# A bias on four token tiles: by matmul or by accumulating transfer, and a shorter form of one scalar step in the norms

## The chip, the cores and the metric

The kernel runs on one core of a Trainium2 chip. The metric is the device time of one execution in microseconds (us). A profile is one such execution taken by the hardware profiler. Its span, from the first to the last instruction, is a little shorter than the execution's own time.

The core has five engines, each with its own queue of instructions in a fixed order: TensorE (PE in the profile; its weight loads are PEld), VectorE (DVE), ScalarE (ACT), GpSimd (POOL) and SyncE (SP). SyncE here issues plain transfers. GpSimd issues the transfers that add to what stands at their destination ("accumulating"). All transfers share 16 DMA engines.

## The reference

One decoder layer over 1024 tokens of width 1024 in fp32: a pooling mixer and a gated feed-forward net with a short convolution, each behind an RMS norm and added to the residual.

```python
def pool_mixer(x, w, b, scale):            # windows 2, 4, 8, 16, one per group of 256 channels
    ...
        groups.append(window_sum / count - xf[..., gi * POOL_GROUP:(gi + 1) * POOL_GROUP])
    d = jnp.stack(groups, axis=2)
    y = jnp.einsum('bsgc,gcd->bsgd', d, w.astype(jnp.float32)).reshape(bsz, seq, D_MODEL) + b
    return (scale * y).astype(x.dtype)

def reference(x, ...):
    h = rms_norm(x, norm_mix_g[layer])
    y = pool_mixer(h, pool_w[j], pool_b[j], pool_scale[j])
    x = x + y.astype(x.dtype)
    f = conv_ffn(rms_norm(x, norm_ffn_g[layer]), ffn_w_in[layer], ffn_conv_w[layer], ffn_conv_b[layer], ffn_w_out[layer])
    x = x + f.astype(x.dtype)
```

What matters here: the mixer adds `scale * b`, the same row of 1024 numbers for every token, to the residual x.

## The kernel before

**Tiles.** The 1024 tokens are 8 tiles of 128 tokens (j = 0 to 7), each a 128 x 1024 fp32 tile `xs[j]` with tokens in the partitions. For each j the mixer stage does, in this order:

- `stat(j)` (through `rstd_of`): ScalarE squares and sums the row (L178, out `junk_a`) and takes a root (L179); VectorE refines it in three steps on one column (L180, L182, L183). L182 computes root * root + ms, with root and ms a column each.
- `mixer_norm(j)`: VectorE scales the four window matrices by that norm (L187, `bandr`).
- `mixer_window(j)` or `window_sums(j)`: 8 matmul calls on `xs[j]` and `bandr` give the window sums, turned so that channels are in the partitions (L201, `psd`). VectorE adds the edges from the tile before (L270), and ScalarE copies the sums out as `dh` (L271).
- `mixer_out(j)`: 8 matmul calls of `dh` with the scaled pool weights `wps` (L286, out `psy`), and two of a tile of ones with `bias_hl`, which holds the scaled bias as a high and a low part in its rows 0 and 1 (L289). VectorE adds x in place (L292, `x1 = psy + x`), SyncE stores x1 to DRAM (L293), and the second norm's `rstd_of` follows (`junk_b`, `st_b`).
- `ffn_norm(j)`: VectorE applies the second norm (L304, out `n`).
- `ffn_operand(j)`: TensorE transposes the result (L319, `pst`); ScalarE and VectorE write it out as high and low parts (L328 to L339).

The fp32 matmul calls of L201 and L286 show as two matmuls each in the profile; the transposes of L319 and the calls on fp32r data (L289, L402) show as one.

**The feed-forward product** is a Strassen-like scheme of seven products per hidden tile n, 22 tiles (L402, banks X, Y, Z). Its weight tile `raws[n]` holds four blocks a11, a12, a21, a22 (`win` in the profile). For each n the scheme needs the sums S3 = a11 + a21, S1 = a21 + a22 (written to a21), S2 = a11 + S1 (written to a11) and S4 = a12 + S2 (written to a12). `sums_in` (L358 to L373) makes them by accumulating transfers on GpSimd (L361, 256 KB each); for n = 0 and 1 it is called with step 0 (S3, S1) and with step 1 (S2, S4). Each operand is split into two parts by ScalarE (L91) and VectorE (L92) before TensorE uses it. From the end of the mixer stage until about 465 us TensorE does these products, then the last product of the layer.

**The order.** Instructions run on each engine in an order fixed when the program is built. It follows the order of the code where operands are ready, and `tc.issue_after(m)` puts a block's instructions behind instruction m in its engine's queue. The loop over j (L527 to L557) holds the mixer's steady part: at step j it issues the window of tile j - 1, the output of tile j - 2, the second norm of j - 2 and the transposes of j - 4. `sums_in(n, 0)` is called at steps 4 and 6, `sums_in(n, 1)` at steps 7 and 8.

**Buffers.** `x_edge`, the 128 rows at the tile edges, is a 128 x 1024 tile with the tag "ha" (one buffer). It is last read by the matmuls of `mixer_edges`. The next user of "ha" is `ha0`, which the products of n = 0 fill.

Of the kernel before, what the change touches and what calls it, by code (L numbers as in the profile page):

```python
# [7 lines left out]
F32 = mybir.dt.float32  # L8
# [3 lines left out]
ALU = mybir.AluOpType  # L12
PSUM = bass.MemoryType.PSUM

P = 128
S = 1024
D = 1024
# [22 lines left out]
NOPS_A = 3  # L40

XBUFS = 5

PAD = 24

# [18 lines left out]
def trunk_kernel(ctx: ExitStack, tc: tile.TileContext, x, consts, par, rows, pool_w, w_in, w_out, out):  # L64
    nc = tc.nc

    const = ctx.enter_context(tc.tile_pool(name="const", bufs=1))
    dram = ctx.enter_context(tc.tile_pool(name="dram", bufs=1, space=bass.MemoryType.DRAM))
# [4 lines left out]
    work = ctx.enter_context(tc.tile_pool(name="work", bufs=1, side="right"))  # L73
# [6 lines left out]
    def bank2(name):  # L80
        return ps_p.tile([P, 2 * NH], F32, tag="ps", name=name)
# [16 lines left out]
    xs = {}  # L98

    def load_x(j):  # L100
        if j < 2 or j >= 2 + XBUFS:
            xs[j] = hls.tile([P, D], F32, tag="hl", name=f"x{j}", bufs=7)
        else:
            xs[j] = pp.tile([P, D], F32, tag="x", name=f"x{j}", bufs=XBUFS)
        for cols in HALVES if j == 0 else [slice(0, D)]:
            nc.sync.dma_start(xs[j][:, cols], x[j * P : (j + 1) * P, cols])
# [28 lines left out]
    for g, w in enumerate(WINDOWS):  # L135

        m = band[:, g, :]
# [30 lines left out]
    def rstd_of(src, name, halves=False):  # L168
        junk = pp.tile([P, D], BF16, tag="junk", name=f"junk_{name}")
        st = pp.tile([P, 8], F32, tag="st", name=f"st_{name}", bufs=8)  # L170
        part, first, ms, root, q, inv, half = (st[:, i : i + 1] for i in range(7))
        bias = eps_t
        if halves:
            bias = first
            nc.scalar.activation(junk[:, :NH], src[:, :NH], AF.Square, accum_out=half)
            nc.vector.tensor_scalar(first, half, D * EPS, None, op0=ALU.add)
            src, junk = src[:, NH:], junk[:, NH:]
        nc.scalar.activation(junk, src, AF.Square, accum_out=part)  # L178
        marks[name] = nc.scalar.activation(root, part, AF.Sqrt, bias=bias).ins  # L179
        nc.vector.tensor_scalar(ms, part, first if halves else D * EPS, None, op0=ALU.add)  # L180

        nc.vector.scalar_tensor_tensor(q, root, root, ms, op0=ALU.mult, op1=ALU.add)  # L182
        nc.vector.reciprocal(inv, q)  # L183
        return root, inv

# [8 lines left out]
    def mixer_norm(j):  # L194
        t = bands[j] = pp.tile([P, NG, P], F32, tag="bandr", name=f"bandr{j}", bufs=2)
        for groups in [slice(0, 2), slice(2, 4)] if j == 0 else [slice(0, NG)]:
            marks[f"band{j}"] = normed(t[:, groups, :], (band if j else band0)[:, groups, :], stats[j])

    def windows(ps, src, weights):
        for c in range(NK):  # L200
            m = nc.tensor.matmul(ps[:, c * P : (c + 1) * P], src[:, c * P : (c + 1) * P], weights[:, c // 2, :], start=True, stop=True)  # L201
        return m.ins
# [13 lines left out]
    wps = pp.tile([P, 2 * NG, GRP], F32, tag="wps", name="wps")  # L216
# [13 lines left out]


    b8 = rows8[:, 1, :]

    def pool_bias():
        marks["bias"] = nc.scalar.activation(bias8[:, 0, :], b8, AF.Copy).ins
        marks["bias_dve"] = nc.vector.tensor_tensor(bias8[:, 1, :], b8, bias8[:, 0, :].bitcast(F32), ALU.subtract).ins
        for l in range(2):
            m = nc.sync.dma_start(bias_hl[l : l + 1, :].bitcast(F32), bias8[:, l, :].bitcast(F32)).ins
        with tc.issue_after(m):
            for j in range(3, NS):  # L240
                load_x(j)
            nc.sync.dma_start(par_sb[:, :GM], par[:, :GM])
# [14 lines left out]
    def window_sums(j):  # L257
        ps = bank2(f"psd{j}")
        marks[f"psd{j}"] = windows(ps, xs[j], bands.pop(j))
        return ps  # L260

    def mixer_window(j, ps=None):
        ps = window_sums(j) if ps is None else ps
        dh = ds[j] = pp.tile([P, NK, P], F32, tag="dh", name=f"dh{j}", bufs=2)
        ps3 = ps.rearrange("p (c s) -> p c s", c=NK)
        first = ps3[:, :, :HALO]
        if j == 0:
            marks["first"] = nc.vector.tensor_tensor(first, first, fac, ALU.mult).ins
        elif j > 1:
            nc.vector.tensor_tensor(first, first, edges[:, :, j * HALO : (j + 1) * HALO], ALU.add)  # L270
        marks[f"dh{j}"] = nc.scalar.activation(dh, ps3, AF.Copy).ins  # L271
# [9 lines left out]
    def mixer_out(j, stats=True):  # L281
        dh = ds.pop(j)
        ps = bank2(f"psy{j}")
        for c in range(NK):
            o = ps[:, c // 2 * GRP : (c // 2 + 1) * GRP]
            nc.tensor.matmul(o, dh[:, c, :], wps[:, c, :], start=c % 4 == 0, stop=False, skip_group_check=True)  # L286
        for h in range(2):
            cols = slice(h * NH, (h + 1) * NH)
            m = nc.tensor.matmul(ps[:, cols], ones, bias_hl[:, cols], start=False, stop=True, skip_group_check=True)  # L289
        marks[f"psy{j}"] = m.ins  # L290
        x1 = n2s[j] = xs.pop(j)
        marks[j] = nc.vector.tensor_tensor(x1, ps, x1, ALU.add).ins  # L292
        nc.sync.dma_start(x1_dram[j * P : (j + 1) * P, :], x1)  # L293
        if stats:
            mixer_out_stats(j)

    def mixer_out_stats(j):
        n2s[j] = (n2s[j], rstd_of(n2s[j], f"b{j}"))

    def ffn_norm(j):  # L300
        x1, r = n2s[j]
        n2 = n2s[j] = pp.tile([P, D], F32, tag="n2", name=f"n2_{j}", bufs=2)
        nc.vector.tensor_tensor(r[1], r[0], r[1], ALU.mult)
        marks[f"n{j}"] = nc.vector.scalar_tensor_tensor(n2, x1, r[1], gains[0], op0=ALU.mult, op1=ALU.mult).ins  # L304
# [50 lines left out]
    def tmp(name):  # L355
        return work.tile([P, NH], F32, tag="sum", name=name, bufs=3)

    def sums_in(n, step):  # L358

        def more(out, a):  # L360
            nc.gpsimd.dma_start(out, a, accum_op=ALU.add)  # L361

        a11, a12, a21, a22 = (raws[n][:, i, k * NH : (k + 1) * NH] for i in range(2) for k in range(2))
        if step == 0:
            s3 = sums[n, "S3"] = tmp(f"S3_{n}")
            nc.sync.dma_start(s3, w_in[order[n]][:, 0, :NH])
            more(s3, a21)
            more(a21, a22)
        else:
            sums[n, "S2"] = a11  # L370
            more(a11, a21)
            sums[n, "S4"] = a12
            more(a12, a11)  # L373
# [95 lines left out]
    def prep_event(k):  # L469
        if k < len(events):  # L470
            n, p = events[k]
            prep_in(n, STEPS[p][0])
# [49 lines left out]
        mixer_edges()  # L522
    with tc.issue_after(marks["edges_pe"]):
        sums3 = window_sums(3)
    with tc.issue_after(marks["dh1+"]), tc.issue_after(marks["edges"]):
        mixer_out_stats(0)
    for j in range(2, NS + 4):  # L527
        if 3 < j < NS:
            with tc.issue_after(marks[1]) if j == 4 else nullcontext():
                mixer_norm(j)  # L530
        if 1 <= j - 1 < NS and j > 2:
            mixer_window(j - 1, {3: sums2, 4: sums3}.get(j))
        if j == NS + 1:
            with tc.issue_after(marks[f"n{NS - 2}"]):
                prep_event(4)
                prep_event(6)
        if 1 <= j - 2 < NS:
            with tc.issue_after(marks["S4", 0] if j == NS + 1 else marks[f"band{min(j, 4)}"]) if j > 2 else nullcontext(), tc.issue_after(marks["psd3"]):
                mixer_out(j - 2)
        if 0 <= j - 2 < NS:  # L540
            with tc.issue_after(marks["dh1+"]):
                ffn_norm(j - 2)
        if 0 <= j - 4 < NS:
            ffn_operand(j - 4)
        if j in (4, 6):
            load_in(j // 2 - 2)
            sums_in(j // 2 - 2, 0)
        if 5 <= j <= 8:
            with tc.issue_after(marks[j - 2]), tc.issue_after(marks[f"b{j - 3}"]):
                prep_event(j - 5)  # L550
        if j in (7, 8):
            sums_in(j - 7, 1)
        if j in (8, 10, 11):
            event((8, 10, 11).index(j))
        with tc.issue_after(marks["edges"]):
            stat(j + 1)
            stat(j + 2)  # L557
# [156 lines left out]
    for k in range(-SLOOK, len(oevents)):  # L714
        p, f = oevents[k + SLOOK] if k + SLOOK < len(oevents) else (None, 0)
# [8 lines left out]
        with tc.issue_after(lasts[-1]) if lasts else nullcontext():  # L724
# [12 lines left out]
            p, f = oevents[k]  # L737
# [10 lines left out]
        if f == 0 and opens:  # L748
            for i in range(4):
                tag = ("XXYY" if set_ == "X" else "YZZZ")[i]  # L750
# [15 lines left out]
        for i, g, c, bank in steps:  # L766
            a, b = oops[p, g]
            alone = opens and (p, i) != ("P4", 3)
            for m, (u, v) in enumerate(((0, 0), (0, 1), (1, 0))):
# [3 lines left out]
                    start=opens and first, stop=g == NP2 - 1 and m == 2, skip_group_check=not alone,  # L773
# [83 lines left out]
```

## Time and profile before

| | us |
|---|---|
| median of 3 runs | 672.28 |
| lowest, highest | 670.89, 673.64 |
| profiled execution, its own time | 670.79 |
| its span | 669.0 |

The TensorE clock that was granted is full speed over the whole span. The rows of the page, of the chain of waits and of the timelines stand in the prediction, where they are used. In a row of a timeline the columns are: start, duration (both us), engine, line, operation, out <- in, shapes, count; in square brackets, how long the engine was idle before it and what released it. In a row of the chain they are: start, duration, engine, tile, line, count. In a row of groups, behind the count, stand the busy time in us, the mean duration of one in ns, and the idle time before them with what ended it. In a row of the windows they are the stretch, its length, and the busy time and count of PE, PEld, DVE, ACT and POOL, then the granted clock, the DMA share and GB/s.

Some stretches of the mixer stage, from the view by windows:

| stretch, us | PE | DVE | ACT | DMA share |
|---|---|---|---|---|
| 20 to 30 | 10.00 | 5.80 | 7.27 | 0.97 |
| 30 to 40 | 10.00 | 9.57 | 8.08 | 0.91 |
| 40 to 50 | 10.00 | 9.26 | 9.53 | 0.82 |
| 50 to 60 | 10.00 | 8.38 | 7.96 | 0.38 |
| 60 to 70 | 10.00 | 9.34 | 5.97 | 0.32 |

### The profile page before, as it was taken

The numbers are of one execution on the slowest core, as the hardware profiler recorded it, in microseconds if no ns is written. First come the engines' busy times: TensorE is split into PE (matmuls) and PEld (weight loads), VectorE is DVE, ScalarE is ACT, GpSimd is POOL, SyncE is SP. The second block draws the span as 40 slices with busy tenths as digits, with TensorE's granted clock in tenths as the row PEclk, the third lists the DMA queues.
The fourth block names the chain that finished last, engine by engine and source line by source line (L and its number), as shares of the span: only waits on it lengthen the run. The fifth ranks groups of instructions, "written<-read, shape, count | busy, mean of one in ns | idle before, by whom it ended". The sixth has DMA issues, their size and how long they took to land.

```text
span 669.0 us, 8720 instructions
## 1 busy us (share of the span) xinstructions
PE 663.6 (99%) x3164; PEld 579.2 (87%) x3164; DVE 569.1 (85%) x841; ACT 338.8 (51%) x517; POOL 47.8 (7%) x73
## 2 busy tenths in 40 slices
PE   9999999999999999999999999999999999999997
PEld 7999878888888888888888888888888888888886
DVE  4798999998888888888888888887987988999995
ACT  6696656554544544444544454454554444444441
POOL 3021020111001111111011101100000000000000
PEclk9999999999999999999999999999999999999999
DMA  8983253544444454544444444429999710232231
GB/s 269 326 207 105 85 141 126 167 145 124 133 134 105 123 142 141 143 130 128 135 141 130 113 136 132 111 92 350 332 335 352 269 58 0 62 96 82 62 125 64
DMA packets 41603, 101.23 MB, mean 151 GB/s; under 512 B 4668, under 2 KB 6616, under 8 KB 38744
## 3 DMA queue, kind: packets, MB, share of 16 engines
q1 hardware_dynamic: 34464, 87.55, 37.3%
q0 software_dynamic: 6944, 12.59, 11.3%
q10 hardware_dynamic: 152, 0.53, 0.3%
q8 instruction: 25, 0.41, 0.2%
q14 instruction: 18, 0.15, 0.1%
HBM read 68.14 MB, written 19.92 MB: 132 GB/s over the span
## 4 chain that ended last, share of the span: by engine, by line
PE 96%; DVE 2%; ACT 1%; issue 0%; POOL 0%; ACTq 0%; POOLq 0%
PE oP L771 29%; PE Y L402 25%; PE X L402 17%; PE Z L402 16%; PE psy L286 4%; PE psd L201 2%; PE pst L319 1%; DVE T L339 1%; PE psy L289 1%; PE ps_scale L222 0%; PE idle_ps L149 0%; DVE n2f L580 0%; ACT B L338 0%; PE ps_edges L201 0%; PE ps_gain L248 0%
## 5 line engine op out<-in xcount | busy, mean ns | idle before, releaser
L771 PE MATMUL oP<-oBP,oAP 128*128 128x512 f32 (+1 forms) x924 | 198.9, 378 | 0.1
L771 PEld LDWEIGHTS oP<-oBP,oAP 128*128 128x128 f32 x924 | 174.0, 189 | 25.0 <-DVE oBP L92 0.5
L402 PE MATMUL X<-B,A11s 128*128 128x512 f32 x264 | 61.5, 380 | 0.0
L402 PE MATMUL Y<-T,S3s 128*128 128x512 f32 x264 | 60.8, 380 | 0.4 <-DVE q L431 0.4
L402 PE MATMUL Y<-T,A22s 128*128 128x512 f32 x264 | 60.8, 380 | 0.0
L402 PE MATMUL Z<-T,S1s 128*128 128x512 f32 x264 | 60.8, 379 | 0.0
L402 PE MATMUL X<-B,A12s 128*128 128x512 f32 x264 | 60.6, 379 | 0.0
L402 PE MATMUL Y<-T,S2s 128*128 128x512 f32 x264 | 60.6, 379 | 0.0
L402 PE MATMUL Z<-B,S4s 128*128 128x512 f32 x264 | 60.5, 379 | 0.0
L402 PEld LDWEIGHTS Y<-T,S3s 128*128 128x128 f32 x264 | 49.7, 189 | 8.2 <-DVE q L431 1.2
L402 PEld LDWEIGHTS Y<-T,A22s 128*128 128x128 f32 x264 | 49.7, 189 | 7.9 <-DVE hb L439 0.6
L402 PEld LDWEIGHTS Z<-T,S1s 128*128 128x128 f32 x264 | 49.8, 189 | 7.5 <-DVE T L339 0.4
L402 PEld LDWEIGHTS Z<-B,S4s 128*128 128x128 f32 x264 | 49.8, 189 | 7.3 <-DVE r L436 0.3
L402 PEld LDWEIGHTS Y<-T,S2s 128*128 128x128 f32 x264 | 49.9, 189 | 7.1
L402 PEld LDWEIGHTS X<-B,A11s 128*128 128x128 f32 x264 | 49.7, 189 | 7.3 <-DVE A11s L92 0.4
L402 PEld LDWEIGHTS X<-B,A12s 128*128 128x128 f32 x264 | 49.8, 189 | 7.0
L91 ACT ACTIVATE oBP<-blk 128x512 fp32r<-128x512 f32 x53 | 33.1, 625 | 44.2 <-PE oP L771 30.6
L460 ACT ACTIVATE gate<-gate 128x1024 f32<-128x1024 f32 x22 | 23.2, 1057 | 49.3 <-DVE gate L451 49.3
L91 ACT ACTIVATE oAP<-blk 128x512 fp32r<-128x512 f32 x55 | 34.1, 620 | 19.3 <-DVE blk L350 16.8
L92 DVE TENSOR_TENSOR oBP<-blk,oBP 128x512 fp32r<-128x512 f32 x53 | 36.5, 688 | 8.6 <-ACT oBP L91 6.6
L92 DVE TENSOR_TENSOR oAP<-blk,oAP 128x512 fp32r<-128x512 f32 x55 | 37.7, 685 | 2.6 <-ACT oAP L91 2.6
L450 DVE SCALAR_TENSOR_TENSOR val<-ha,par_sb,val 128x1023 f32<-128x1023 f32 x22 | 28.2, 1283 | 13.2 <-ACT val L449 13.2
(131 smaller groups left out, 958.3 us busy)
## 6 DMA issues: line engine op xcount, KB each, us to landing
win<-in_w_in_dram SPq DMA_DIRECT2D x22, 1024.0 KB, 4.8
g_dram<-val SPq DMA_DIRECT2D x22, 512.0 KB, 2.6
blk<-g_dram SPq DMA_DIRECT2D x33, 256.0 KB, 5.2
blk<-in_w_out_dram SPq DMA_DIRECT2D x31, 256.0 KB, 5.7
win<-win POOLq DMA_DIRECT2D x26, 256.0 KB, 3.5
S<-in_w_in_dram SPq DMA_DIRECT2D x22, 256.0 KB, 3.5
S<-win POOLq DMA_DIRECT2D x22, 256.0 KB, 4.2
A12s<-g_dram SPq DMA_DIRECT2D x22, 256.0 KB, 5.2
```

Source lines behind the costliest of these rows:

```text
L91: nc.scalar.activation(t[:, 0, :], src, AF.Copy)
L92: m = nc.vector.tensor_tensor(t[:, 1, :], src, t[:, 0, :].bitcast(F32), ALU.subtract)
L201: m = nc.tensor.matmul(ps[:, c * P : (c + 1) * P], src[:, c * P : (c + 1) * P], weights[:, c // 2, :], start=True, stop=True)
L286: nc.tensor.matmul(o, dh[:, c, :], wps[:, c, :], start=c % 4 == 0, stop=False, skip_group_check=True)
L289: m = nc.tensor.matmul(ps[:, cols], ones, bias_hl[:, cols], start=False, stop=True, skip_group_check=True)
L319: nc.tensor.transpose(ps[:, c * P : (c + 1) * P], n2[:, c * P : (c + 1) * P], ident)
L339: return hi, nc.vector.tensor_tensor(l, src, h.bitcast(F32), ALU.subtract).ins
L402: nc.tensor.matmul(bank, a[:, i, ks], woven(b[:, l, k, :]), start=opens and m == 0, stop=m == 11, skip_group_check=not opens)
L450: nc.vector.scalar_tensor_tensor(t[:, 1:], src[:, : S - 1], w[1], t[:, 1:], op0=ALU.mult, op1=ALU.add)
L460: nc.scalar.activation(gate, gate, AF.Silu)
L771: nc.tensor.matmul(bank, a[:, u, i * P : (i + 1) * P], woven(b[:, v, :])[:, c.start // 2 : c.stop // 2, :], start=opens and first, stop=g ...
```

## The change

For tiles 0 to 3 nothing changes in `mixer_out`. For tiles 4 to 7 the two bias matmuls are left out. In their place the scaled bias row, `b8`, is written to a row in DRAM, read back over all 128 partitions into a tile of the tag "ha" (`bias_spread`, issued behind the edge matmuls), and added to `xs[j]` by an accumulating transfer on GpSimd (`bias_into`) after the window of that tile and before L292 reads it. The transfer a21 += a22 of n = 0 and 1 is taken out of step 0 of `sums_in` and is issued, as step 2, behind the transfers to tiles 4 and 5. For n > 1 `sums_in` does the same as before.

In `rstd_of`, root * root + ms is one `tensor_scalar` whose two scalars are the columns root and ms, where it was a `scalar_tensor_tensor` with one column of scalars and ms as a tensor of one column. It runs 17 times: 8 times for the first norm, 8 times for the second, once for the edges.

```diff
+BY_DMA = 4
...
-        nc.vector.scalar_tensor_tensor(q, root, root, ms, op0=ALU.mult, op1=ALU.add)
+        nc.vector.tensor_scalar(q, root, root, ms, op0=ALU.mult, op1=ALU.add)
...
+    bias_row = dram.tile([1, D], F32, tag="bias_row", name="bias_row")
+    biased = {}
+
+    def bias_spread():
+        biased["tile"] = work.tile([P, D], F32, tag="ha", name="bias_b", bufs=1)
+        nc.gpsimd.dma_start(biased["tile"], bias_row.to_broadcast([P, D]))
+
+    def bias_into(j):
+        if j >= BY_DMA:
+            biased[j] = nc.gpsimd.dma_start(xs[j], biased["tile"], accum_op=ALU.add).ins
...
         marks["bias_dve"] = nc.vector.tensor_tensor(bias8[:, 1, :], b8, bias8[:, 0, :].bitcast(F32), ALU.subtract).ins
+        nc.gpsimd.dma_start(bias_row.rearrange("o (k p) -> (o k) p", p=P), b8)
...
-            nc.tensor.matmul(o, dh[:, c, :], wps[:, c, :], start=c % 4 == 0, stop=False, skip_group_check=True)
-        for h in range(2):
+            m = nc.tensor.matmul(
+                o, dh[:, c, :], wps[:, c, :], start=c % 4 == 0, stop=j >= BY_DMA and c % 4 == 3, skip_group_check=True
+            )
+        for h in range(0 if j >= BY_DMA else 2):
             cols = slice(h * NH, (h + 1) * NH)
             m = nc.tensor.matmul(ps[:, cols], ones, bias_hl[:, cols], start=False, stop=True, skip_group_check=True)
...
             more(s3, a21)
+        if step == 0 and n > 1 or step == 2:
             more(a21, a22)
-        else:
+        if step == 1:
             sums[n, "S2"] = a11
...
         sums3 = window_sums(3)
+        bias_spread()
...
             mixer_window(j - 1, {3: sums2, 4: sums3}.get(j))
+            bias_into(j - 1)
...
             sums_in(j // 2 - 2, 0)
+        if j in (5, 6):
+            with tc.issue_after(biased[j - 1]):
+                sums_in(j - 5, 2)
```

## The prediction

> **What bounds the kernel now.** I read the page first (shares, then the chain), then the chain in order of time around the token tiles that change, then the timelines of VectorE, TensorE, GpSimd and ScalarE over the same stretch.
>
> ```profile
> span 669.0 us, 8720 instructions
> ...
> PE 663.6 (99%) x3164; PEld 579.2 (87%) x3164; DVE 569.1 (85%) x841; ACT 338.8 (51%) x517; POOL 47.8 (7%) x73
> ...
> PE 96%; DVE 2%; ACT 1%; issue 0%; POOL 0%; ACTq 0%; POOLq 0%
> ```
>
> The chain that ends last is TensorE for 96% of the span, so time comes out if TensorE instructions go and nothing else steps into their place. The chain in order of time shows those that go:
>
> ```profile
> 43.30 0.46 PE psy L289 x2
> ...
> 49.98 0.47 PE psy L289 x2
> ...
> 56.56 0.46 PE psy L289 x2
> ...
> 63.94 0.46 PE psy L289 x2
> 64.41 1.75 PE pst L319 x16
> ```
>
> These are the pairs of bias matmuls of tiles 4 to 7. All four pairs are on the chain, with TensorE work directly before and after each. What follows them:
>
> ```profile
> 66.15 5.40 PE X L402 x25
> ...
> 71.58 1.08 PE pst L319 x8
> ...
> 72.68 0.61 ACT n2f L331
> ...
> 73.31 0.70 DVE n2f L350
> ...
> 89.27 0.61 DVE q L431
> ...
> 89.93 4.15 PE Y L402 x18
> ```
>
> At 71.58 tile 7 is transposed, ScalarE copies it out, and from there to 89.88 the chain runs over ScalarE and mostly VectorE. Then it is TensorE to the end. So the lead must be handed on at 71.58, and VectorE must start its long stretch earlier by the same amount.
>
> **The change part by part.**
>
> *The removed matmuls.* Four tiles lose two matmuls each: 0.46 + 0.47 + 0.46 + 0.46 = 1.85 us, if all of it reaches 71.58. That cross-checks against the step of ordinary work of this width:
>
> ```profile
> 126.40 2.59 PE Z L402 x12
> ```
>
> Twelve 128x512 matmuls take 2.59 us, 0.216 each, so eight are 1.73 us. I take 1.85 and keep 1.73 as the other end. The Trainium skill ("TensorE: Matmul & The Clock Gate", "Back-to-back issue gap") gives about 131 ns per matmul of 512 columns in a stream with weight loads; by it the sum would be 8 x 0.131 = 1.05 us. This trace has 216 ns for such a stream, and the measurement decides.
>
> *Does the lead get through VectorE?* Each tile's matmuls are followed by VectorE's add x1 = psy + x (L292). Its rows, with the idle time in front:
>
> ```profile
> 44.56 1.22 DVE L292 TENSOR_TENSOR x<-psy,x 128x1024 f32<-128x1024 f32 x1
> ...
> 50.48 1.22 DVE L292 TENSOR_TENSOR x<-psy,x 128x1024 f32<-128x1024 f32 x1 [0.30 <-PE psy L289]
> ...
> 57.06 1.22 DVE L292 TENSOR_TENSOR x<-psy,x 128x1024 f32<-128x1024 f32 x1 [0.96 <-PE psy L289]
> ...
> 64.44 1.22 DVE L292 TENSOR_TENSOR x<-psy,x 128x1024 f32<-128x1024 f32 x1 [0.53 <-PE psy L289]
> ...
> 70.15 1.28 DVE L304 SCALAR_TENSOR_TENSOR n<-x,st_b,gain_b 128x1024 f32<-128x1024 f32 x1
> ```
>
> For tile 4 VectorE is late already: its matmuls end at 43.76 and the add begins at 44.56. For tiles 5, 6 and 7 VectorE waits 0.30, 0.96 and 0.53 us. So the lead goes through only as far as VectorE can arrive earlier too. Part of that comes from the other edit, L182:
>
> ```profile
> L182 DVE SCALAR_TENSOR_TENSOR st_a<-st_a 128x1 f32<-128x1 f32 x8 | 1.7, 218 | 1.3 <-ACT st_a L179 0.5 <-DVE st_a L180 0.5
> L182 DVE SCALAR_TENSOR_TENSOR st_b<-st_b 128x1 f32<-128x1 f32 x8 | 1.7, 214 | 1.1 <-ACT st_b L179 1.1
> ...
> L180 DVE TENSOR_SCALAR st_a<-st_a 128x1 f32<-128x1 f32 x8 | 1.3, 158 | 3.3 <-ACT junk_a L178 3.3
> ```
>
> The new form is a TENSOR_SCALAR of one column. The nearest row is L180, 158 ns (with one constant instead of two columns), so each refinement saves 0.06 us; the other end is nothing. Of these, 17 in all, about six lie between 30 us and the add of tile 5, that is 0.36 us.
>
> Now tile by tile. Add 5: TensorE is done 0.93 earlier (two pairs), at 49.5; VectorE arrives at 50.48 - 0.30 - 0.36 = 49.8. VectorE decides: 0.66 gained. Add 6: TensorE 57.02 - 1.39 = 55.6; VectorE 57.06 - 0.96 - 0.66 - 0.06 = 55.4. TensorE decides: 1.39 gained. Add 7: TensorE 64.41 - 1.85 = 62.56; VectorE 64.44 - 0.53 - 1.39 - 0.06 = 62.46. TensorE decides by a tenth: 1.85 gained. If the refinement saves nothing, VectorE arrives at add 5 with 0.30, at add 6 with 1.26, and at add 7 at 62.65: 1.79 instead of 1.85. So the second edit matters little, and neither end of its price moves the sum by more than 0.1. From add 7 the norm of tile 7 (L304, 70.15 to 71.43) releases the transposes at 71.58; the 25 matmuls in between end at 71.55, so both arms arrive together and both have moved.
>
> *VectorE from 73.31 on.* It has no refinement left there and runs nearly full (windows):
>
> ```profile
> 72.66:89.93 17.27, 16.86 (x78) 14.07 (x77) 16.52 (x21) 10.38 (x14) 1.33 (x2) 1.00 0.40 120
> 89.93:126.40 36.47, 36.45 (x163) 30.41 (x164) 36.27 (x45) 22.57 (x29) 3.84 (x5) 1.00 0.47 132
> ```
>
> The third busy column is VectorE: 16.52 of 17.27 us and 36.27 of 36.47. Nothing is added or removed there, so the stretch keeps its length and shifts with its start.
>
> *The added transfers.* On GpSimd's queue six DMAs are added: a 4 KB row to DRAM, its spread over 128 partitions (512 KB), and four accumulates of 512 KB. Two accumulates of 256 KB (a21 += a22 for n = 0, 1) move behind those of tiles 4 and 5. Nothing is added on SP. Each accumulate may start when the window sums of its tile have read x:
>
> ```profile
> 31.13 1.95 PE L201 MATMUL psd<-bandr,x 128*128 128x128 f32 x16
> ...
> 37.80 2.05 PE L201 MATMUL psd<-bandr,x 128*128 128x128 f32 x16
> ...
> 44.48 2.05 PE L201 MATMUL psd<-bandr,x 128*128 128x128 f32 x16
> ...
> 51.15 1.95 PE L201 MATMUL psd<-bandr,x 128*128 128x128 f32 x16
> ```
>
> They end at 33.1, 39.8, 46.5 and 53.1, less the lead of 0, 0, 0.46 and 0.93. The adds that need the result come at 44.3 (44.56 less some refinements), 49.8, 55.6 and 62.6. Room: 11.2, 10.0, 9.6 and 10.4 us. No row shows an accumulate of 512 KB; the nearest are these:
>
> ```profile
> win<-win POOLq DMA_DIRECT2D x26, 256.0 KB, 3.5
> ...
> q0 software_dynamic: 228, 0.41, 49.3%
> q1 hardware_dynamic: 144, 0.52, 26.4%
> ...
> q1 hardware_dynamic: 540, 1.74, 97.6%
> ...
> win<-in_w_in_dram SPq DMA_DIRECT2D x2, 1024.0 KB, 9.5
> ```
>
> The middle two are 40 to 45 us, the last two 20 to 25 us. In the former 228 packets of about 2 KB took 49.3% of 16 x 5 engine us, 0.173 each; 512 KB are 256 of them, 44 engine us, 2.8 us over 16 engines, against 1.4 for 256 KB. So I take 3.5 + 1.4 = 4.9 us to land; the ends are 3.5 and the 9.5 of a 1 MB load in the fullest stretch. Even 9.5 fits the narrowest room. Cost nothing, then, hidden by the window's copy-out and the main matmuls; if that cover goes, the add waits the excess. The spread moves 0.52 MB; at the rate of the 20 to 25 row (1.74 MB in 4.9 us) that is 1.5 us more for loads in flight.
>
> **Sum.** 1.85 us gained; 1.7 with both lower ends (1.73 for the matmuls, 0.06 less through VectorE). The profiled execution took 670.79 us (span 669.0), so 668.9; the median of the runs shown is 672.28, 1.5 above it, so 670.4 there. About 0.5%, 3.4 us, is what a measurement of this kernel tells from no change.
>
> **The rivals.**
>
> *Slower: a late operand on GpSimd's queue.* An in-order queue gains a waiting instruction per tile, and all later sums stand behind it.
>
> ```profile
> 52.60 0.86 POOL L361 DMA_DIRECT2D win<-win  x1 [5.07 <-DVE A12s L92]
> ...
> 56.47 0.64 ACT L91 ACTIVATE S4s<-win 128x512 fp32r<-128x512 f32 x1
> 57.94 0.60 ACT L331 ACTIVATE n2f<-pst 128x512 f32<-128x512 f32 x1 [0.83 <-PE pst L319]
> 58.43 1.06 ACT L178 ACTIVATE junk_b<-x 128x1024 bf16<-128x1024 f32 x1
> ```
>
> The sum a12 += a11 for n = 0 is issued at 52.60, lands 3.3 to 3.5 us later, near 56, and ScalarE's split S4s starts at 56.47: half a microsecond of slack. If the accumulate of tile 7 (ready at 52.2) is issued first, it transfers from 53.1 to 55.9, the sum behind it to 57.3, and with the 1.2 us that 3.5 leaves beside 0.9 of issue and 1.4 of transfer it lands near 58.5. S4s then holds ScalarE, the square sum of tile 6 (58.43 before) starts at 59.5 behind two steps that take their places in 0.5 us each, and VectorE reaches add 7 as long after it as before (63.91 - 58.43 = 5.48 us, less 0.06), at 64.9 instead of 64.44: +0.5 us, 672.8. The point from which it is slower than before is a start of S4s at 58.0 (59.0 for the square sum, less the 0.53 that VectorE waited). For it: slack is short and the transfer engines are over 70% full from 40 to 45. Against: the sum's own operand is ready at 52.3, about when the accumulate is, and comes first in the program.
>
> *VectorE absorbs the lead.* If VectorE only reaches add 7 at its old time, the wait of 0.53 is all that is won: 671.7. For it: the margin at add 7 is a tenth. Against: the lead at tiles 5 and 6 moves VectorE too.
>
> *The matmuls were covered and nothing moves*, so the change does not do what it says: 672.3. The Trainium skill ("Perfetto Trace Analysis", "Identifying the Most-Contended Engine") says matmul busy time is no good measure of room on TensorE and points to weight loads, 87% here. Against, from rows: the chain's matmuls stand at equal steps with no waits.
>
> *More than the matmuls.* Between 89.93 and 126.40, 163 matmuls took 36.47 us; at 0.216 they are 35.2. A different interleaving could win those 1.3 us besides: 669.2.
>
> **How the numbers follow.** Forecast (gain 1.2 to 2.5 us) 0.50; slower by a late operand 0.18; absorbed by VectorE 0.14; nothing moves 0.05; more 0.08; an upset of the order that costs more than 3.4 us 0.05. The likeliest is the forecast, 670.4 us, and its own range is 669.4 to 671.4. The whole range is 668.8 to 674.2: below, the case of more, with the spread of a median; above, the late operand with about a microsecond beyond its price. Faster by over 0.5% (under 668.9) needs the case of more plus spread: 0.10. Slower by over 0.5% (above 675.6) is the upset, or a late operand at twice the price: 0.09. Within: 0.81.
>
> **What would show it.** Right: no L289 rows for tiles 4 to 7; the add of tile 7 near 62.6 with a wait on TensorE; the tile 7 transposes near 69.7; the step from VectorE back to TensorE near 88.1; L182 as TENSOR_SCALAR near 158 ns; accumulates of 512 KB landing within 5 to 6 us. Wrong: an L292 that waits for a DMA (accumulate late); S4s waiting for a DMA past 58.0 (late operand); no wait before the last two adds (VectorE absorbed it); a chain that leaves TensorE elsewhere (the order upset).

## The result and the profile after

| | us |
|---|---|
| before, median of 6 runs | 671.18 |
| after, median of 6 runs | 676.56 |
| ratio after / before, with its 95% interval | 1.0071 (1.0051 to 1.0092) |
| profiled execution after: its own time, its span | 675.10, 673.4 |

The change makes the kernel slower by 0.7%, where 0.3% faster was forecast (670.4 us, in a range of 668.8 to 674.2). Line numbers after L43 have moved: the splits L91 and L92 are now L93 and L94, L182 is L184, L201 L203, L286 L299, L289 L304, L292 L307, L319 L334, L361 L376, L402 L418, and the accumulates of the bias are L244.

First the page of the changed kernel: span, busy time by engine, and the share of the chain that ended last.

```profile
span 673.4 us, 8722 instructions
...
PE 661.9 (98%) x3156; PEld 576.7 (86%) x3156; DVE 569.5 (85%) x841; ACT 338.9 (50%) x517; POOL 52.2 (8%) x79
...
PE 85%; DMA 6%; DVE 4%; ACT 3%; issue 1%; SPq 0%; POOL 0%; ACTq 0%; DVEq 0%; POOLq 0%
```

TensorE is busy 1.7 us less, as it should be with eight matmuls gone, and yet the span is 4.4 us longer. The chain, 96% TensorE before, now has 6% of transfers and more of VectorE and ScalarE. In order of time (start, duration, what) the pieces that matter are these:

```profile
46.26 6.76 DMA win<-win
...
54.62 7.78 DMA win<-win
...
62.42 0.63 ACT S4s L93
...
68.92 1.15 DVE x L307
...
75.97 1.08 PE pst L334 x8
...
94.33 4.15 PE Y L418 x18
```

The tile 7 add stands at 68.9 where it was at 64.4, tile 7's transposes at 75.97 where they were at 71.58, and the return to TensorE at 94.33 where it was at 89.93: 4.4 us at each place. The whole loss arises before the add of tile 7, and nothing is won or lost after. Of the 4.4, 0.3 is there already when the window sums of tile 4 start (31.47, where it was 31.13). The traces of the kernels below scatter at that place, from 30.6 to 32.3, with no order by what was changed. So the times of two traces can differ by some tenths, once by 1.2 us, for no reason in the change, and a stretch counted from that place says more. The chain names its origin: two transfers on GpSimd's queue. That queue's timeline (start, duration of the issue, line, out <- in, and in brackets how long GpSimd was idle before and what released it):

```profile
33.97 0.87 POOL L244 DMA_DIRECT2D x<-bias_b  x1 [1.27 <-DMA win<-in_w_in_dram]
36.67 0.85 POOL L376 DMA_DIRECT2D win<-win  x1 [1.84 <-DVE st_a L182]
39.23 0.85 POOL L376 DMA_DIRECT2D S<-win  x1 [1.71 <-DMA S<-in_w_in_dram]
44.15 0.90 POOL L376 DMA_DIRECT2D win<-win  x1 [4.07 <-DVE st_a L184]
44.69 1.24 POOL L244 DMA_DIRECT2D x<-bias_b  x1
46.26 0.85 POOL L376 DMA_DIRECT2D win<-win  x1 [0.33 <-DMA S<-win]
53.55 0.86 POOL L376 DMA_DIRECT2D win<-win  x1 [6.45 <-DMA win<-win]
54.09 1.21 POOL L244 DMA_DIRECT2D x<-bias_b  x1
54.62 1.56 POOL L376 DMA_DIRECT2D win<-win  x1
55.16 1.91 POOL L244 DMA_DIRECT2D x<-bias_b  x1
```

Read with the code, these are, in the same order (win0 and win1 are the weight tiles of n = 0 and 1, x4 to x7 the token tiles):

```
x4 += bias;  win0: a21 += a22 (S1);  S3_1 += a21;  win0: a11 += a21 (S2);  x5 += bias;
win1: a21 += a22 (S1);  win1: a11 += a21 (S2);  x6 += bias;  win0: a12 += a11 (S4);  x7 += bias
```

TensorE's window sums of tiles 5 and 6 stand here:

```profile
38.08 2.04 PE L203 MATMUL psd<-bandr,x 128*128 128x128 f32 x16
...
44.60 2.05 PE L203 MATMUL psd<-bandr,x 128*128 128x128 f32 x16
```

The accumulate of tile 6 could have gone at 46.5, when its window sums were done (the next group follows at 46.48). It stands behind the S2 sum of n = 1, which waits until 53 for the S1 sum of n = 1 to land. It is issued at 54.09. Tile 5's stands behind the S2 sum of n = 0, which goes at 44.15: ready at 40.0, issued at 44.69. Then four transfers go out within 1.6 us, and what the next steps need of them lands late. VectorE's adds of tiles 5, 6 and 7:

```profile
51.78 1.23 DVE L307 TENSOR_TENSOR x<-psy,x 128x1024 f32<-128x1024 f32 x1 [1.58 <-DMA x<-bias_b]
...
61.22 1.23 DVE L307 TENSOR_TENSOR x<-psy,x 128x1024 f32<-128x1024 f32 x1 [3.77 <-DMA x<-bias_b]
...
68.84 1.22 DVE L307 TENSOR_TENSOR x<-psy,x 128x1024 f32<-128x1024 f32 x1
```

ScalarE's steps ahead of tile 6's second norm:

```profile
62.42 0.63 ACT L93 ACTIVATE S4s<-win 128x512 fp32r<-128x512 f32 x1 [4.54 <-DMA win<-win]
...
63.44 1.05 ACT L180 ACTIVATE junk_b<-x 128x1024 bf16<-128x1024 f32 x1
```

Two waits run side by side. The add of tile 6 ends at 62.45, because its accumulate (54.09) lands 7.1 us after its issue. S4s begins at 62.42, because the S4 sum of n = 0 (54.62) lands 7.8 us after its issue. The square sum of tile 6 (`junk_b`) needs both, the add as its operand and ScalarE free of S4s. It begins at 63.44 where it was at 58.43. VectorE's norm of tile 6, two splits and the add of tile 7 follow in that order. Of the 5.0 us, VectorE's old wait of 0.53 ahead of that add takes up a part, and 4.4 remain.

The other edit shows in the groups (count, then busy us and mean ns):

```profile
L184 DVE TENSOR_SCALAR st_a<-st_a 128x1 f32<-128x1 f32 x8 | 2.2, 272 | 1.2 <-ACT st_a L181 0.5 <-DVE st_a L182 0.5
L184 DVE TENSOR_SCALAR st_b<-st_b 128x1 f32<-128x1 f32 x8 | 2.2, 269 | 1.1 <-ACT st_b L181 1.1
...
L182 DVE TENSOR_SCALAR st_a<-st_a 128x1 f32<-128x1 f32 x8 | 1.3, 159 | 2.6 <-ACT junk_a L180 2.6
```

The one operation with two columns of scalars takes 270 ns, not the 158 of its neighbour with one constant, and more than the 216 of the form that it replaces.

### The profile page after: what moved, and what is told of

It is laid out like the page before. It is cut to its first block, busy times and chain, and to the rows that moved or that the text cites. A ratio compares the mean times of both kernels' runs of the same rounds, so it can differ in the third digit from the quotient of the medians.

```text
span 673.4 us, 8722 instructions
## 1 busy us (share of the span) xinstructions
PE 661.9 (98%) x3156; PEld 576.7 (86%) x3156; DVE 569.5 (85%) x841; ACT 338.9 (50%) x517; POOL 52.2 (8%) x79
## 4 chain that ended last, share of the span: by engine, by line
PE 85%; DMA 6%; DVE 4%; ACT 3%; issue 1%; SPq 0%; POOL 0%; ACTq 0%; DVEq 0%; POOLq 0%
PE oP L792 29%; PE Y L418 25%; PE X L418 15%; PE Z L418 15%; DMA win<-win 2%; DMA x_edge<-in_x_dram 1%; DMA S<-win 1%; DMA S<-in_w_in_dram 1%; DMA x<-in_x_dram 1%; DVE T L354 1%; ACT junk_b L180 1%; DVE x L307 1%; DVE n L319 0%; DVE n2f L601 0%; ACT junk_a L180 0%
## 5 line engine op out<-in xcount | busy, mean ns | idle before, releaser
L418 PE MATMUL X<-B,A11s 128*128 128x512 f32 x264 | 61.5, 380 | 0.0
L418 PE MATMUL Y<-T,S3s 128*128 128x512 f32 x264 | 60.8, 380 | 0.4 <-DVE q L447 0.4
L418 PE MATMUL Y<-T,A22s 128*128 128x512 f32 x264 | 60.9, 380 | 0.0
L418 PE MATMUL Z<-T,S1s 128*128 128x512 f32 x264 | 60.8, 379 | 0.0
L418 PE MATMUL X<-B,A12s 128*128 128x512 f32 x264 | 60.7, 379 | 0.0
L418 PE MATMUL Y<-T,S2s 128*128 128x512 f32 x264 | 60.6, 379 | 0.0
L418 PE MATMUL Z<-B,S4s 128*128 128x512 f32 x264 | 60.5, 379 | 0.0
L418 PEld LDWEIGHTS Y<-T,S3s 128*128 128x128 f32 x264 | 49.7, 189 | 8.2 <-DVE q L447 1.2
L418 PEld LDWEIGHTS Y<-T,A22s 128*128 128x128 f32 x264 | 49.7, 189 | 7.9 <-DVE hb L455 0.6
L418 PEld LDWEIGHTS Z<-T,S1s 128*128 128x128 f32 x264 | 49.8, 189 | 7.5 <-DVE T L354 0.4
L418 PEld LDWEIGHTS Z<-B,S4s 128*128 128x128 f32 x264 | 49.8, 189 | 7.3 <-DVE r L452 0.3
L418 PEld LDWEIGHTS Y<-T,S2s 128*128 128x128 f32 x264 | 49.9, 189 | 7.1
L418 PEld LDWEIGHTS X<-B,A11s 128*128 128x128 f32 x264 | 49.7, 189 | 7.3 <-DVE A11s L94 0.4
L418 PEld LDWEIGHTS X<-B,A12s 128*128 128x128 f32 x264 | 49.8, 189 | 7.0
L93 ACT ACTIVATE oBP<-blk 128x512 fp32r<-128x512 f32 x53 | 33.1, 625 | 44.2 <-PE oP L792 30.6
L93 ACT ACTIVATE oAP<-blk 128x512 fp32r<-128x512 f32 x55 | 34.1, 620 | 19.3 <-DVE blk L365 16.8
L94 DVE TENSOR_TENSOR oBP<-blk,oBP 128x512 fp32r<-128x512 f32 x53 | 36.5, 689 | 8.6 <-ACT oBP L93 6.6
L94 DVE TENSOR_TENSOR oAP<-blk,oAP 128x512 fp32r<-128x512 f32 x55 | 37.8, 686 | 2.6 <-ACT oAP L93 2.6
```

The lines of the kernel that those rows point to most:

```text
L93: nc.scalar.activation(t[:, 0, :], src, AF.Copy)
L94: m = nc.vector.tensor_tensor(t[:, 1, :], src, t[:, 0, :].bitcast(F32), ALU.subtract)
L418: nc.tensor.matmul(bank, a[:, i, ks], woven(b[:, l, k, :]), start=opens and m == 0, stop=m == 11, skip_group_check=not opens)
```

## The experiments

Three theories. **Q:** the order of GpSimd's queue; accumulates stand behind sums that wait, are issued late, and what needs them waits. **T:** traffic; 2 MB of accumulates fill the transfer engines in any order. **N:** the norms' new form. Every ratio is against runs of the kernel before on the same chip.

| kernel | median us | ratio (95% interval) |
|---|---|---|
| dma_only | 675.65 | 1.0069 (1.0052 to 1.0086) |
| norm_only | 671.15 | 1.0007 (0.9997 to 1.0017) |
| no_bias | 669.45 | 0.9983 (0.9974 to 0.9993) |
| ordered | 671.51 | 1.0008 (0.9999 to 1.0018) |
| x5_first | 673.57 | 1.0039 (1.0026 to 1.0052) |
| x6_first | 673.73 | 1.0043 (1.0029 to 1.0056) |
| s4_vector | 676.99 | 1.0089 (1.0074 to 1.0104) |
| tiles67 | 670.92 | 0.9998 (0.9989 to 1.0007) |
| ordered_old_norm | 670.99 | 0.9999 (0.9989 to 1.0008) |
| ordered2 | 670.71 | 0.9995 (0.9985 to 1.0005) |
| s4_later | 669.90 | 0.9976 (0.9965 to 0.9987) |
| before_s4_later | 670.99 | 1.0004 (0.9991 to 1.0018) |

**The two edits apart: dma_only and norm_only.** The first is the changed kernel with the old line, the second the kernel before with the new one.

```diff
-        nc.vector.tensor_scalar(q, root, root, ms, op0=ALU.mult, op1=ALU.add)
+        nc.vector.scalar_tensor_tensor(q, root, root, ms, op0=ALU.mult, op1=ALU.add)
```

> The changed kernel with the old form of the norms' refinement (scalar_tensor_tensor, one column of scalars); the transfers stay. Theory Q (GpSimd's queue: the accumulates of tiles 5 and 6 stand behind sums that wait, so they are issued late and the adds and the S4 split wait for them): the loss stays, 4 to 5.5 us over the kernel before, and the two adds wait 4 to 6 us together. Theory N (the loss is the new scalar form, 270 ns where the old took 216): the loss goes, within 1 us of before. If N only adds to Q, up to 0.9 us comes off, 17 x 0.055.

> The kernel before with the new form of the refinement alone. Theory Q: within 0.5 us of before, since 17 x 0.055 = 0.9 us of VectorE lies mostly beside TensorE; the form takes 270 ns here too. Theory N: 3 us or more slower than before.

The loss stays with the transfers alone (1.0069, and the two adds wait 5.1 us together), and the new form alone gives 1.0007, an interval that holds no change. In norm_only's groups the form is as dear as in the changed kernel:

```profile
L182 DVE TENSOR_SCALAR st_a<-st_a 128x1 f32<-128x1 f32 x8 | 2.2, 271 | 1.3 <-ACT st_a L179 0.5 <-DVE st_a L180 0.5
```

So the dearer form is real and lies mostly beside TensorE. Theory N falls as the cause.

**The removed matmuls alone: no_bias.** The kernel before, without the bias of tiles 4 to 7.

```diff
...
-        for h in range(2):
+        for h in range(0 if j >= 4 else 2):
```

> The kernel before without the two bias matmuls of tiles 4 to 7 and with nothing in their place: the bias of those tiles is left out. If the term for the removed matmuls was right, 1.7 to 1.9 us faster than before (ratio near 0.997), with the add of tile 7 near 62.6. If the matmuls were covered or VectorE absorbs the lead: 0 to 0.6 us.

0.9983: by the ratio 1.1 us faster, between 0.5 and 1.7. Its timeline of VectorE, adds of tiles 6 and 7:

```profile
55.47 1.22 DVE L292 TENSOR_TENSOR x<-psy,x 128x1024 f32<-128x1024 f32 x1 [0.50 <-PE psy L286]
...
62.39 1.23 DVE L292 TENSOR_TENSOR x<-psy,x 128x1024 f32<-128x1024 f32 x1
```

the step of its chain back to TensorE:

```profile
87.86 4.15 PE Y L402 x18
```

and on TensorE the window sums of tile 4, which stand ahead of the first matmul that is gone:

```profile
30.62 1.95 PE L201 MATMUL psd<-bandr,x 128*128 128x128 f32 x16
```

The add of tile 7 is 2.05 us earlier than before and so is the return to TensorE (87.86 against 89.93). But 0.51 of it is there at the window sums of tile 4 (30.62 against 31.13), before any matmul is missing, and isn't the matmuls' gain. From these window sums to the add of tile 7 it takes 31.8 us, where the kernel before takes 33.3 (33.2 and 33.1 in norm_only and before_s4_later, which have all their matmuls). So a lead of about 1.5 us goes through, and VectorE does not eat it. That lies inside the interval of the times, 0.5 to 1.7, and the forecast's 1.85 lies just outside it. The Trainium skill's 131 ns per streamed matmul of 512 columns ("TensorE: Matmul & The Clock Gate", "Back-to-back issue gap") would give 1.05 us, as an estimate. The total cannot tell it from eight steps of 216 ns, 1.73 us, but the step itself is 216 ns in the trace of the kernel before, and the 1.5 us is nearer to the larger.

**The order of the queue: ordered, x5_first, x6_first.** In ordered three edges put the accumulate of tile 5 ahead of the S2 sum of n = 0, that of tile 6 ahead of the S2 sum of n = 1, and the S4 sum of n = 0 ahead of it as well. The other two have one of the edges each.

```diff
...
         if step == 1:
             sums[n, "S2"] = a11
-            more(a11, a21)
+            with tc.issue_after(biased[5 + n]), tc.issue_after(marks["s4"]) if n else nullcontext():
+                more(a11, a21)
             sums[n, "S4"] = a12
-            more(a12, a11)
+            marks["s4"] = more(a12, a11)
```

> The changed kernel with the order of GpSimd's queue changed: the accumulate of tile 5 ahead of the S2 sum of n = 0, that of tile 6 ahead of the S2 sum of n = 1, and the S4 sum of n = 0 ahead of the S2 sum of n = 1. The same transfers and bytes. Theory Q: the adds wait little and the matmuls' gain shows: 1 to 2 us faster than before, 6 to 7 faster than the changed kernel. Theory T (the 2 MB of accumulates fill the transfer engines and land 7 us late in any order): 674 us or more, with S4s still waiting 3 us or more for its sum.

> The changed kernel with one edge in GpSimd's queue: the S2 sum of n = 1 goes behind the accumulate of tile 6. Tile 5's accumulate still stands behind the S2 sum of n = 0. If the late issue of tile 6 carries most of the loss: 672 to 673.5 us, the wait of the add of tile 6 (3.8 us) gone, that of tile 5 (1.6) still there. If traffic does it: 675 us or more.

> The changed kernel with one edge: the S2 sum of n = 0 goes behind the accumulate of tile 5. Tile 6's accumulate still stands behind the S2 sum of n = 1, which waits for the S1 sum of n = 1 to land. The wait of the add of tile 5 goes; if tile 6 carries most of the loss, its wait stays above 3 us and the time is 674.5 us or more.

In ordered, GpSimd's accumulates of tiles 5 and 6, and VectorE's add of tile 6:

```profile
40.59 1.01 POOL L244 DMA_DIRECT2D x<-bias_b  x1
...
46.99 1.55 POOL L244 DMA_DIRECT2D x<-bias_b  x1
```

```profile
56.19 1.23 DVE L307 TENSOR_TENSOR x<-psy,x 128x1024 f32<-128x1024 f32 x1 [0.44 <-PE psy L299]
```

The transfers and bytes are the same, tile 6's accumulate goes at 47 instead of 54, no add waits for a transfer in this execution, and the loss is gone (1.0008). Yet each still takes long to land (issue to landing of the four):

```profile
DMA to landing us min/median/max: 7.6/7.7/8.6
```

So T is right about the landing and wrong about the price: 7.7 us fit into the room of 9.6 to 11.2 that the windows leave, if the issue is on time. With one edge alone somewhat less than half of the loss goes, 1.0043 and 1.0039. In x6_first, VectorE's adds of tiles 5 and 6 and ScalarE's S4s:

```profile
52.16 1.23 DVE L307 TENSOR_TENSOR x<-psy,x 128x1024 f32<-128x1024 f32 x1 [2.06 <-DMA x<-bias_b]
...
57.75 1.22 DVE L307 TENSOR_TENSOR x<-psy,x 128x1024 f32<-128x1024 f32 x1
```

```profile
62.08 0.63 ACT L93 ACTIVATE S4s<-win 128x512 fp32r<-128x512 f32 x1 [3.82 <-DMA win<-win]
```

In x5_first:

```profile
49.53 1.22 DVE L307 TENSOR_TENSOR x<-psy,x 128x1024 f32<-128x1024 f32 x1
...
58.18 1.23 DVE L307 TENSOR_TENSOR x<-psy,x 128x1024 f32<-128x1024 f32 x1 [2.98 <-DMA x<-bias_b]
```

```profile
60.48 0.63 ACT L93 ACTIVATE S4s<-win 128x512 fp32r<-128x512 f32 x1 [4.85 <-DMA win<-win]
```

In each, the tile that was put first no longer waits, and the S4 sum is still late. In x6_first it alone holds what follows: the add of tile 6 begins 3.5 us earlier than in the changed kernel, the add of tile 7 (68.49) only 0.35. The expectation that tile 6's late issue carries most of the loss missed: x6_first stayed above its range of 672 to 673.5, and x5_first came out below 674.5. The ordered kernel missed as well, since the matmuls' gain did not show.

**Is it the adds or S4s? s4_vector.** The S4 sum of n = 0 leaves the queue and is an add on VectorE.

```diff
         if step == 1:
             ...
-            sums[n, "S4"] = a12
-            more(a12, a11)
+            if n:
+                sums[n, "S4"] = a12
+                more(a12, a11)
```

> The changed kernel with one sum taken off GpSimd's queue: S4 of n = 0 (a12 += a11) is an add on VectorE (0.7 us). The accumulates of tiles 5 and 6 still stand behind waiting sums. If the wait of S4s (4.5 us on ScalarE) is what holds the chain: 671 to 672 us. If the adds of tiles 5 and 6, which wait for their accumulates (1.6 and 3.8 us), hold it alone as well: 674 us or more, with those waits unchanged.

```profile
52.80 1.22 DVE L307 TENSOR_TENSOR x<-psy,x 128x1024 f32<-128x1024 f32 x1 [2.81 <-DMA x<-bias_b]
...
61.58 1.22 DVE L307 TENSOR_TENSOR x<-psy,x 128x1024 f32<-128x1024 f32 x1 [3.11 <-DMA x<-bias_b]
...
66.00 1.28 DVE L319 SCALAR_TENSOR_TENSOR n<-x,st_b,gain_b 128x1024 f32<-128x1024 f32 x1
```

1.0089, and the adds (VectorE's timeline) still wait, 5.9 us together where it was 5.3. The last row is the norm of tile 6: 66.00, against 66.43 in the changed kernel and 61.43 before. So the adds hold the chain without any late S4 sum, and taking away only the wait that ended last, by a microsecond, buys next to nothing. (Behind that norm VectorE also bears the new add here, and the split S4s now waits for it, so the time itself is not the price of the adds alone.)

**Half the bytes: tiles67.** Transfers for tiles 6 and 7 only.

```diff
-BY_DMA = 4
+BY_DMA = 6
...
-            with tc.issue_after(biased[j - 1]):
+            with tc.issue_after(biased[j - 1]) if j - 1 >= BY_DMA else nullcontext():
```

> The changed kernel with the transfers for tiles 6 and 7 alone; tiles 4 and 5 keep their matmuls, and the order of the queue is left as it falls. Half the bytes. Theory Q: tile 6's accumulate stands behind the S2 sum of n = 1, which is ready earlier here (no accumulate of tile 5 in front of its operand), so most of the loss goes: 671 to 673 us. Theory T: half of the loss, 673 to 674.

0.9998, a little better than either expected. Tile 6's accumulate still stands behind the S2 sum of n = 1, but this goes at 47.57, not 53.55 (GpSimd's timeline):

```profile
47.57 0.84 POOL L376 DMA_DIRECT2D win<-win  x1 [2.08 <-DMA win<-win]
48.10 1.19 POOL L244 DMA_DIRECT2D x<-bias_b  x1
```

It waited for the landing of the S1 sum of n = 1. In the changed kernel that sum had tile 5's accumulate before it in the same queue and took 6.8 us to land; here it is issued at 43.8 or later and has landed by 47.6, within 3.8 us. So order and traffic are not apart: the accumulate lengthens the landing of a sum, the next sum's wait for that landing holds the queue, and the next accumulate stands behind it.

**What holds back the gain in ordered? ordered_old_norm, ordered2, s4_later, before_s4_later.** The first is ordered with the old form of the refinement. The second has the old form too and moves the S2 sum of n = 0 forward besides, so that the S4 sum's operand lands sooner (step 1 of `sums_in` is split: step 3 issues a11 += a21, step 1 the rest):

```diff
             with tc.issue_after(biased[j - 1]):
-                sums_in(j - 5, 2)
+                if j == 6:
+                    sums_in(0, 3)
+                with tc.issue_after(marks["s2", 0]) if j == 6 else nullcontext():
+                    sums_in(j - 5, 2)
...
+            if j == 8:
+                with tc.issue_after(marks["s4", 0]), tc.issue_after(biased[6]):
+                    sums_in(1, 3)
             sums_in(j - 7, 1)
```

> The reordered kernel with the old form of the refinement. Theory Q with a small N: 0.2 to 0.9 us faster than the reordered kernel, since VectorE arrives late at the adds there; if the form is hidden, no difference.

> As the reordered kernel, and besides the S2 sum of n = 0 ahead of the S1 sum of n = 1, the S2 sum of n = 1 behind the S4 sum of n = 0, and the old form of the refinement. Theory Q (S4s waited 1.26 us there because its own chain of sums stood behind others): S4s waits 0.3 us or less, and the time is 0.8 to 1.8 us faster than before. Theory T (traffic): S4s waits 1 us or more still, within 0.5 us of the reordered kernel.

Neither gets the gain, 0.9999 and 0.9995, and ordered2 missed the 0.8 to 1.8 us that theory Q gave it. The old form may be worth half a microsecond (0.9999 against 1.0008), but the two intervals overlap. In ordered_old_norm's execution the add of tile 6 waits for its accumulate after all (VectorE's timeline), so the order leaves little room:

```profile
55.55 1.23 DVE L307 TENSOR_TENSOR x<-psy,x 128x1024 f32<-128x1024 f32 x1 [0.59 <-DMA x<-bias_b]
```

In ordered2, ScalarE's S4s and VectorE's add of tile 7:

```profile
58.08 0.63 ACT L93 ACTIVATE S4s<-win 128x512 fp32r<-128x512 f32 x1 [0.96 <-DMA win<-win]
```

```profile
64.44 1.22 DVE L307 TENSOR_TENSOR x<-psy,x 128x1024 f32<-128x1024 f32 x1
```

The S4 sum is issued at 53.13, as soon as its operand is split, and lands 5 us later (3.3 to 3.5 before); tile 6's accumulate, issued at 47.82, is in front of it in the queue. Here theory T has its part: S4s still waits 0.96 us, and the add of tile 7 no longer waits for TensorE. That it stands at 64.44, as before the change, is in part chance: in this execution the window sums of tile 4 start at 32.33, 1.2 us later than before, and from there to the add it takes 32.1 us, 1.2 less than before. So the last step, added to ordered2, takes away not the delay but the need: on VectorE the split of the S4 sum of n = 0 goes behind tile 7's norm, where the kernel before has a wait of 1.28 us, and on ScalarE S4s goes behind tile 6's square sum (56.86, then S4s at 59.45), less far than the expectation says.

```diff
                 prep_event(4)
-                prep_event(6)
...
-            with tc.issue_after(marks["S4", 0] if j == NS + 1 else marks[f"band{min(j, 4)}"]) ...
+            with tc.issue_after(marks["S1", 0] if j == NS + 1 else marks[f"band{min(j, 4)}"]) ...
...
-        if k not in (4, 6):
+        if k != 4:
```

> The second reordered kernel, with the S4 split of n = 0 moved on ScalarE and VectorE from ahead of tile 7's add to behind tile 7's norm. If the late landing of the S4 sum (S4s waits 0.96 us there) is what still holds back the gain of the matmuls: 669.0 to 669.9 us, 1 to 2 us faster than before, add of tile 7 near 62.7. If something else holds it: as the second reordered kernel, 670.7.

> The control: the kernel before with only that move of the S4 split. S4s waits for nothing there, so the move by itself should bring nothing: within 0.5 us of before. If it brings 1 us or more, the move and not the transfers is the gain.

0.9976: 1.6 us faster than before, between 0.9 and 2.3, and the move alone, without the transfers, gives 1.0004. Its adds of tiles 6 and 7 on VectorE:

```profile
55.49 1.23 DVE L307 TENSOR_TENSOR x<-psy,x 128x1024 f32<-128x1024 f32 x1 [0.50 <-PE psy L299]
...
62.43 1.23 DVE L307 TENSOR_TENSOR x<-psy,x 128x1024 f32<-128x1024 f32 x1 [0.69 <-PE psy L299]
```

Both wait for TensorE again, as the forecast had it. The add of tile 7 stands 2.0 us earlier than in the kernel before, of which 0.4 are there at the window sums of tile 4 (30.71), so 1.6 remain. The accumulates land no sooner than in the slow kernel (7.0 to 9.8 us there):

```profile
DMA to landing us min/median/max: 8.0/8.6/9.4
```

This version beats both kernels. It has the old form of the refinement. What its last step alone is worth stays open: from tile 4's window sums to the add of tile 7 it takes 0.4 us less than in ordered2, and the intervals of the two ratios overlap by a hair.

## Why the prediction was wrong

**The term for the matmuls was right in mechanism and somewhat large.** 1.85 us was forecast. no_bias and s4_later show 1.5 and 1.6 us between tile 4's window sums and tile 7's add, and 1.1 and 1.6 us by their ratios. Where the other 0.3 goes stays open. VectorE lets the lead through, as worked out tile by tile, and the stretch from tile 7's transposes on shifts whole.

**The step that failed is "Cost nothing, then", in the part on the added transfers.** It compared the time to land with the room from the end of the window sums to the add, as if each accumulate were issued at the end of its window sums. Tile 6's was issued 7.6 us after that and tile 5's 4.7. Their waits on VectorE follow from the issue and not from the length of the transfer: in ordered, s4_later and the changed kernel alike they land 7 to 10 us after the issue, and of these only in the last does an add wait. Two of the signs that the prediction gave for being wrong came: an add waiting for a transfer (1.58 and 3.77 us), and S4s waiting past 58.0 (until 62.42). The prediction listed the queue's instructions but did not put them in order and give each its own release. Had it done so, the S2 sum of n = 1 would have shown: it needs the S1 sum of n = 1, which the change itself moves behind tile 5's accumulate.

**The landing was mis-sized.** 4.9 us was taken, 7.6 is the median. The transfer's own 2.8 us held, as far as an estimate goes: from 56 to 62 us the engines are full (DMA share, the last but one column), and at 197 GB/s 512 KB take 2.7 us. The count of packets behind the 2.8 did not hold: from 30 to 75 us GpSimd's queue carries 1152 packets before, for eight transfers of 256 KB, and 1728 after, with four of 512 KB besides. That is 144 for each of either size, so the larger transfer has larger packets and not more of them. By bytes the sum comes out the same.

```profile
56.00:62.00 6.00, 6.00 (x33) 5.34 (x32) 2.20 (x3) 1.89 (x3) 1.07 (x2) 1.00 1.08 197
```

What was missing is the transfers in front of it and beside it; how much each adds, no run takes apart. The Trainium skill ("DMA: Bandwidth & Descriptors", "Anatomy of one DMA") fits 2.0 us plus bytes over 436 GB/s for one transfer from GpSimd's queue; by that, 512 KB would be estimated at 3.2 us. No run here shows such an accumulate alone, and in the three runs whose landings are given here every one took more than twice that.

**The slower rival named the right place and the wrong instruction.** It had the S4 sum behind tile 7's accumulate, at +0.5 us. It was tile 6's accumulate and the S4 sum, both behind the S2 sum of n = 1, at +4.4 in the profile and 5.4 in the medians. It was given 0.18, an upset of the order that costs this much 0.05, and the range ended at 674.2.

**The refinement was priced from the wrong neighbour.** The row of a TENSOR_SCALAR with one constant gave 158 ns, and the other end of the range was the old 216. The form with two columns of scalars takes 270, outside both ends. It decided nothing here.

## What to carry to other kernels

A transfer added to an in-order queue is priced by what stands in front of it: write the queue down in its order, give each entry the time at which its own operand is ready, and only then compare the landing with the room. If an accumulate lengthens the landing of a sum on which a later entry of the same queue waits, the delay comes round again. Where two late operands meet at one instruction, an experiment that takes away one of them can show little or nothing; undo both, or move the consumer away.

## What the runs showed of the hardware

A VectorE operation on one column takes 270 ns as tensor_scalar whose two scalars are columns (272 and 269 in the changed kernel, 271 in norm_only), 216 ns as scalar_tensor_tensor with one column of scalars (218 and 214 in the kernel before), and 158 ns as tensor_scalar with one constant. That the form with one tensor operand less is the dearest of the three was not expected.

A late operand can cost TensorE its clock as well as the wait. In dma_only's profiled execution TensorE waits 3.61 us for tile 6's norm (until 68.59), and the page's row of the granted clock, in tenths over 40 slices of 16.9 us, dips in the fifth:

```profile
PEclk9999799999999999999999999999999999999999
```

The windows of 70 to 74 us show 0.50 of full speed. From the add of tile 7 to the return to TensorE it takes 26.5 us there, and 25.5 in the kernel before and in the changed kernel's profile, where the same wait was 3.29 us and the clock stayed full. Five of the changed kernel's six executions have a mean clock of 0.995 to 0.997, and the profiled one 1.000. This may be the microsecond by which the medians lose more than the profile (5.4 against 4.4); it is not shown, since the others have no trace.
